# Softmax on negated scores in a windowed-attention encoder kernel on one Trainium2 core

## The chip, the cores and the metric

The kernel runs on one core of one Trainium2 chip. A core has five engines, each with an instruction queue that is worked off in order: TensorE (PE in the profile; its weight loads are shown apart as PEld) multiplies matrices into PSUM, VectorE (DVE) and ScalarE (ACT) do elementwise work and can read PSUM, GpSimd (POOL) does elementwise work on SBUF, and SyncE (SP) issues the transfers. Engines wait for one another through semaphores. The metric is the device time of one execution in microseconds; lower is better.

## The reference

One layer of a hybrid encoder is applied to two batches with the same weights: a prompt of 512 tokens and a sample of 1024 tokens, 1024 channels, float32. After an RMSNorm, one projection gives queries, keys and values for eight heads of 64 channels (two key/value heads, four query heads each) and the inputs of a convolution module. The two branches are joined, projected and added to the input; then comes a gated feed-forward part with 2816 inner channels and a final RMSNorm.

The change lies in the attention. For each block of 128 queries, the keys are those of the block itself and of its neighbours on both sides (384 keys, 256 at the ends of the sequence). Each head has a learned sink logit, which takes part in the softmax's maximum and sum but has no value row:

```
sc = einsum(q, k) * HEAD_DIM ** -0.5 + bias        # bias: relative position, by head
sc = where(|q - k| <= 128, sc, -1e30)
m = maximum(max(sc), sink)
p = exp(sc - m)
denom = sum(p) + exp(sink - m)
o = (p / denom) @ v
```

## The kernel before

All large products are made in a split form: an operand is stored as a rounded high part and the remainder, and three products are added (`hi*hi`, `hi*lo`, `lo*hi`). Making these pairs is most of the work of ACT (the cast to the high part) and of DVE and POOL (the subtraction): `split`, L140 to L145, does it for weights, L211 and L212 for normalised inputs, L548 and L549 for the attention's probabilities.

The program is written as a sequence of stages, partly as generators that are interleaved:

- The prompt's input projections come first, then the sample's. Beside the sample's projections runs the prompt's attention (`prompt`, from about 119 to 250 us), with the depthwise convolution of 31 taps (`conv_items`, L269 to L304, on DVE at L289 and L293, with some taps on ACT at L282 and L285 and POOL at L286).
- The prompt's feed-forward part follows (`ffn_step`; up-projection through `proj`, L250, L251 and L253; three-tap convolution with L775 and L779; gate at L793 to L798; down-projection L813 to L816). Beside it runs the sample's attention (`sample`, from about 400 to 755 us).
- From about 900 us the sample's feed-forward part follows, as products in seven terms over half-size blocks (`prod`, L1039, and `mm_down`, L1352).

`tick` (L228) sets how many steps of a side generator are taken between groups of matmuls, by the rates `RA` to `RE`. This fixes the order in which instructions are given; up to the last stage, a planner then works out each engine's order from the instructions' dependences, their order of writing and estimated durations. In the last stage (from L1202) the order on PE is the written one, and near its end that of SP too.

Attention goes by units: 12 blocks of 128 queries (4 of the prompt, 8 of the sample) times two key/value heads make 24 units of four heads each. A unit's `scores` (L485) takes, for each of its four heads, two matmuls of the scores into a PSUM bank (L502); then one DVE operation (L505) adds the bias, writes the sum to an SBUF tile and leaves the row maximum in a column of `mx`. In the profile L505 shows as a CUSTOM operation and a short read of the accumulator. Then follow, for the four heads together, the negative of the maximum of `mx` and the sink (L512, `negm`) and the sink's exponent (L513, `es`), both on DVE; the four exponentials with `negm` as a bias column, which also leave the row sums in `den` (L515, ACT); the sink's exponential for the four heads in one operation (L517, ACT); the sum of `den` and `es` (L518) and its reciprocal (L519) on DVE; and the scaling of the four tiles on ACT (L523) or on POOL or DVE (L525). `values` (L534) transposes the probabilities on PE (L546), splits them (L548 on ACT, L549 on DVE), multiplies by the values (L560, L561) and stores the result with L568 to L572.

`sinkb` holds the eight sink logits in every partition, `nsink` their negatives; both are made once at the beginning. The small columns (`mx`, `negm`, `den`, `es`) come from a set of 32 small buffers that are given out in turn.

Of the kernel before, what the change touches and what calls it, by code (L numbers as in the profile page):

```python
# [12 lines left out]
AF = mybir.ActivationFunctionType  # L13
ALU = mybir.AluOpType
# [8 lines left out]
GRP = NH // NKV  # L23
# [73 lines left out]
def tile_hybrid_encoder(ctx: ExitStack, tc: tile.TileContext, xs, rel_bias, norm_attn_g, w_in,  # L97
                        attn_sink, conv_dw_w, conv_dw_b, conv_ln_g, conv_ln_b, w_out, norm_ffn_g,
                        w_up, ffn_dw_w, ffn_dw_b, w_down, norm_final_g, onehot, outs):
    nc = tc.nc  # L100
# [11 lines left out]
    def sm(n):  # L112
        return sb.tile([n])

    def bank(job):
        return banks.tile([NT], among=use[job])
# [289 lines left out]
    sinkb = cst.tile([P, NH], F32, name="sinkb")  # L406
    nsink = cst.tile([P, NH], F32, name="nsink")
# [49 lines left out]
    bias = []  # L457
# [15 lines left out]
    def load_q(u):  # L473
        if u < 2 * NB and u not in qt:
            q = sb.tile([GRP, P], F32R)
            i, kv = divmod(u, 2)
            nt, b = divmod(i, 4)
            nc.sync.dma_start(q[:].bitcast(F32), qsd[nt][b, :, kv * GRP:(kv + 1) * GRP, :])
            qt[u] = q

    def window(i):
        G, b = blocks[i]
        return [k for k in (b - 1, b, b + 1) if 0 <= k < G["nb"]]

    def scores(u):  # L485
        i, kv = divmod(u, 2)
        load_q(u)
        if blocks[min(u + 1, 2 * NB - 1) // 2][0] is blocks[i][0]:
            load_q(u + 1)
        G, b = blocks[i]  # L490
        kts = window(i)
        k0, nk = kts[0] * P, len(kts) * P
        off = (kts[0] - b + 1) * P
        q = qt.pop(u)
        mx, negm, den, es = sm(GRP), sm(GRP), sm(GRP), sm(GRP)
        hs = slice(kv * GRP, (kv + 1) * GRP)
        pr = []
        for j in range(GRP):
            h = kv * GRP + j
            sc = bank("attn")  # L500
            for L in range(2):
                nc.tensor.matmul(sc[:, :nk], q[:, j, :], kt[G["g"], kv][L][:, k0:k0 + nk],  # L502
                                 start=(L == 0), stop=(L == 1))
            p = sb.tile([3 * P])
            nc.vector.tensor_tensor_reduce(  # L505
                out=p[:, :nk], in0=sc[:, :nk], in1=bias[h][:, off:off + nk], scale=1.0,
                scalar=-3.0e38, op0=ALU.add, op1=ALU.max, accum_out=mx[:, j:j + 1])
            pr.append(p)
            del sc
            if j == 1:  # L510
                yield 0.0
        nc.vector.scalar_tensor_tensor(negm[:], mx[:], -1.0, nsink[:, hs], op0=ALU.mult, op1=ALU.min)  # L512
        nc.vector.tensor_tensor(es[:], sinkb[:, hs], negm[:], op=ALU.add)  # L513
        for j in range(GRP):
            nc.scalar.activation(pr[j][:, :nk], pr[j][:, :nk], AF.Exp, bias=negm[:, j:j + 1],  # L515
                                 accum_out=den[:, j:j + 1])
        nc.scalar.activation(es[:], es[:], AF.Exp)  # L517
        nc.vector.tensor_tensor(den[:], den[:], es[:], op=ALU.add)  # L518
        nc.vector.reciprocal(den[:], den[:])  # L519
        for j in range(GRP):  # L520
            eng = (SCB if G["g"] == 0 else SCD)[j]
            if eng == "a":
                nc.scalar.activation(pr[j][:, :nk], pr[j][:, :nk], AF.Identity, scale=den[:, j:j + 1])  # L523
            else:
                (nc.vector if eng == "v" else nc.gpsimd).tensor_scalar_mul(pr[j][:, :nk], pr[j][:, :nk], den[:, j:j + 1])  # L525
        units[u] = pr
        yield 0.0
# [51 lines left out]
    def attention(u0, u1, then={}):  # L579
        yield from scores(u0)  # L580
        for u in range(u0, u1):
            if u + 1 < u1:
                yield from scores(u + 1)
            yield from values(u)
            if u in then:
                yield from then[u]
# [698 lines left out]
    pr, second_half = {}, {}  # L1285
# [284 lines left out]
```

## Time and profile before

| what | value |
|---|---|
| median of 3 runs | 1562.63 us (1561.66 to 1564.55) |
| the profiled execution | 1563.92 us, span 1562.1 us |
| granted TensorE clock | 0.998 |
| PE / DVE / ACT / POOL busy | 97% / 77% / 51% / 47% of the span |
| instructions | 20200 |

The span goes from the first to the last instruction of the profiled execution. In rows of the profile, `L505` is line 505 of the kernel; `h<-a,h` names the tiles written and read with their numbers left out; `x24` counts instructions; after the bar stand busy microseconds, the mean of one in ns, and the idle time of the engine just before them with what ended it. In rows of waits, `PE a L561 <- DVE h L549: 1.7, 3, 1.2` says that L561 on PE waited for L549 on DVE 1.7 us in all, three times, at most 1.2 us. In rows in order of time, the first number is the start and the second the duration. A matmul's shown duration overlaps the next one's.

### The profile page before, as it was taken

To read this page: it belongs to the slowest core of one execution; us is meant where nothing else is said; L and a number is where in the kernel's file an instruction comes from. 1 tells how busy PE (TensorE), PEld (TensorE's weight loads), DVE (VectorE), ACT (ScalarE), POOL (GpSimd) and SP (SyncE) were. 2 spreads that over 40 slices of the span, in tenths; PEclk is the share of its full clock that TensorE was granted. 3 is DMA by queue.
4 is the path that set the end of the run, shared out by engine and by line. 5 is a ranking of instruction groups with operands and counts; after the bars stand their busy time and mean duration, and the time that the engine had idled before them with its cause. 6 is when DMAs were issued, how large, how long until landed. Compare 5 with 4: busy or idle time off the path is not lost. (4 is left out here: it accounts for less than half of the span.)

```text
span 1562.1 us, 20200 instructions
## 1 busy us (share of the span) xinstructions
PE 1519.2 (97%) x6909; PEld 1234.5 (79%) x6909; DVE 1200.5 (77%) x1731; ACT 799.2 (51%) x1426; POOL 729.5 (47%) x559
## 2 busy tenths in 40 slices
PE   8899899999998999999999999999999999999998
PEld 6787788887886778888877887888888878788886
DVE  7999868638989996756675768777777777877795
ACT  4634566335565655656554455444444445544364
POOL 7651344238576676656653324555555554000135
PEclk9999999999999999999999999999999999999999
DMA  7573246446331333333657222333333332694642
GB/s 229 157 201 95 87 118 165 130 133 166 108 117 64 108 108 109 99 97 95 212 164 230 82 68 78 111 102 101 101 102 102 101 102 101 206 354 144 219 142 108
DMA packets 209771, 207.62 MB, mean 133 GB/s; under 512 B 11156, under 2 KB 150748, under 8 KB 209541
## 3 DMA queue, kind: packets, MB, share of 16 engines
q1 hardware_dynamic: 209669, 206.35, 42.0%
q8 instruction: 54, 0.88, 0.2%
q14 instruction: 48, 0.39, 0.1%
HBM read 158.84 MB, written 48.51 MB: 133 GB/s over the span
## 5 line engine op out<-in xcount | busy, mean ns | idle before, releaser
L144 POOL TENSOR_TENSOR q<-q,q 128x1024 fp32r<-128x1024 f32 x72 | 175.0, 2436 | 68.8 <-ACT q L143 33.8
L921 POOL TENSOR_TENSOR q<-q,q 128x512 fp32r<-128x512 f32 x82 | 114.0, 1401 | 155.9 <-ACT q L1031 151.4
L250 PE MATMUL u<-h,q 128*128 128x512 f32 x400 | 158.5, 396 | 3.6 <-DVE h L775 2.8
L251 PE MATMUL u<-h,q 128*128 128x512 f32 x400 | 158.6, 396 | 0.6 <-DVE h L212 0.6
L253 PE MATMUL u<-h,q 128*128 128x512 f32 x384 | 151.9, 396 | 2.2 <-POOL q L144 2.2
L1045 PE MATMUL w<-h,q 128*128 128x512 f32 x372 | 147.4, 396 | 3.1 <-ACT h L1126 1.7
L1047 PE MATMUL w<-h,q 128*128 128x512 f32 x372 | 145.9, 392 | 0.6 <-POOL q L921 0.6
L293 DVE SCALAR_TENSOR_TENSOR c<-c,cvw,c 128x512 f32<-128x512 f32 x184 | 138.1, 750 | 2.4
L1046 PE MATMUL w<-h,q 128*128 128x512 f32 x350 | 137.6, 393 | 0.0
L143 ACT CAST q<-q 128x1024 fp32r<-128x1024 f32 x72 | 75.6, 1050 | 77.5 <-POOL q L144 44.6
L918 POOL TENSOR_TENSOR q<-q,q 128x1024 f32<-128x1024 f32 x8 | 23.8, 2989 | 182.9 <-DVE q L918 171.2
L250 PE MATMUL b<-h,q 128*128 128x512 f32 x256 | 102.1, 399 | 2.9 <-DVE d L323 2.9
L1354 PE MATMUL w<-h,h 128*128 128x512 f32 x264 | 103.8, 393 | 0.0
L1356 PE MATMUL w<-h,h 128*128 128x512 f32 x264 | 103.6, 392 | 0.0
L921 DVE TENSOR_TENSOR h<-h,h 128x512 fp32r<-128x512 f32 (+1 forms) x128 | 92.3, 764 | 11.4 <-ACT h L925 9.2
L251 PE MATMUL b<-h,q 128*128 128x512 f32 x256 | 100.7, 393 | 0.0
L253 PE MATMUL b<-h,q 128*128 128x512 f32 x256 | 100.5, 393 | 0.0
L1355 PE MATMUL w<-h,h 128*128 128x512 f32 x244 | 95.9, 393 | 0.0
L921 POOL TENSOR_TENSOR c<-q,c 128x512 fp32r<-128x512 f32 x46 | 71.0, 1557 | 51.8 <-ACT c L1031 51.8
L250 PEld LDWEIGHTS u<-h,q 128*128 128x128 f32 x400 | 75.6, 189 | 20.4 <-DVE h L775 3.3
L925 ACT CAST h<-h 128x512 fp32r<-128x512 f32 x101 | 58.7, 618 | 59.4 <-DVE h L921 27.0
L251 PEld LDWEIGHTS u<-h,q 128*128 128x128 f32 x400 | 75.5, 189 | 16.4 <-DVE h L212 1.6
(457 smaller groups left out, 4278.8 us busy)
## 6 DMA issues: line engine op xcount, KB each, us to landing
q<-in_w_up SPq DMA_DIRECT2D x88, 512.0 KB
h<-in_w_down SPq DMA_DIRECT2D x90, 256.0 KB
ga<-q SPq DMA_DIRECT2D x64, 256.0 KB
h<-ga SPq DMA_DIRECT2D x57, 256.0 KB
q<-in_w_in SPq DMA_DIRECT2D x28, 512.0 KB
q<-in_x_sample SPq DMA_DIRECT2D x15, 512.0 KB
h<-qsd SPq DMA_DIRECT2D x24, 256.0 KB
q<-ga SPq DMA_DIRECT2D x20, 256.0 KB
```

Source lines behind the costliest of these rows:

```text
L144: (nc.vector if dve else nc.gpsimd).tensor_tensor(lo[:], raw[:], hi[:].bitcast(F32), op=ALU.subtract)
L250: nc.tensor.matmul(out, whi[:, kc, :], hi[:], start=(kc == 0), stop=False)
L251: nc.tensor.matmul(out, whi[:, kc, :], lo[:], start=False, stop=False)
L253: nc.tensor.matmul(out, wlo[:, kc, :], hi[:], start=False, stop=(kc == KC - 1))
L293: nc.vector.scalar_tensor_tensor(acc[:], src(t), w(t), acc[:], op0=ALU.mult, op1=ALU.add)
L921: (eng or nc.vector).tensor_tensor(out, a, b, op=ALU.subtract)
L1045: nc.tensor.matmul(out, whi[:, s], hi[:], start=(start and c == 0), stop=False, **go)
L1046: nc.tensor.matmul(out, whi[:, s], lo[:], start=False, stop=False, **go)
L1047: nc.tensor.matmul(out, wlo[:, s], hi[:], start=False, stop=(stop and c == 3), **go)
L1354: nc.tensor.matmul(out, sh[:, c], th[:], start=(p == 0), stop=False)
L1355: nc.tensor.matmul(out, sh[:, c], tl[:], start=False, stop=False)
L1356: nc.tensor.matmul(out, sl[:, c], th[:], start=False, stop=(p == NPAIR - 1))
```

## The change

The row operation now takes the scores with the sign turned: `out = (scores + bias) * -1`, and instead of a running maximum from a large negative constant it keeps a running minimum that starts from the head's column of `nsink`. What it leaves is therefore already the minimum of the negated scores and the negated sink, the value that `negm` had; it goes into a column of `negm`, and `mx` and L512 are gone. The exponential takes its input with a factor of -1. The sink's exponent is no longer added up on DVE (L513 is gone); instead, ScalarE makes `exp(sink + negm)` with a bias column, once for each head, as four one-column operations in place of one of four columns. The sum, the reciprocal and the scaling stay as they were.

```diff
-        mx, negm, den, es = sm(GRP), sm(GRP), sm(GRP), sm(GRP)
-        hs = slice(kv * GRP, (kv + 1) * GRP)
+        negm, den, es = sm(GRP), sm(GRP), sm(GRP)
...
             nc.vector.tensor_tensor_reduce(
-                out=p[:, :nk], in0=sc[:, :nk], in1=bias[h][:, off:off + nk], scale=1.0,
-                scalar=-3.0e38, op0=ALU.add, op1=ALU.max, accum_out=mx[:, j:j + 1])
+                out=p[:, :nk], in0=sc[:, :nk], in1=bias[h][:, off:off + nk], scale=-1.0,
+                scalar=nsink[:, h:h + 1], op0=ALU.add, op1=ALU.min, accum_out=negm[:, j:j + 1])
...
-        nc.vector.scalar_tensor_tensor(negm[:], mx[:], -1.0, nsink[:, hs], op0=ALU.mult, op1=ALU.min)
-        nc.vector.tensor_tensor(es[:], sinkb[:, hs], negm[:], op=ALU.add)
+
         for j in range(GRP):
-            nc.scalar.activation(pr[j][:, :nk], pr[j][:, :nk], AF.Exp, bias=negm[:, j:j + 1],
+            nc.scalar.activation(pr[j][:, :nk], pr[j][:, :nk], AF.Exp, scale=-1.0, bias=negm[:, j:j + 1],
                                  accum_out=den[:, j:j + 1])
-        nc.scalar.activation(es[:], es[:], AF.Exp)
+        for j in range(GRP):
+            h = kv * GRP + j
+            nc.scalar.activation(es[:, j:j + 1], sinkb[:, h:h + 1], AF.Exp, bias=negm[:, j:j + 1])
         nc.vector.tensor_tensor(den[:], den[:], es[:], op=ALU.add)
```

## The prediction

> **What bounds the kernel now.** I read the page first, then busy time by stage, then what TensorE waited for in those stages, and only then the rows of the changed lines. The page gives the engines' shares:
>
> ```profile
> span 1562.1 us, 20200 instructions
> PE 1519.2 (97%) x6909; PEld 1234.5 (79%) x6909; DVE 1200.5 (77%) x1731; ACT 799.2 (51%) x1426; POOL 729.5 (47%) x559
> ```
>
> TensorE is the bound: only 1562.1 - 1519.2 = 42.9 us of the span are left on it. The softmax runs from 119.5 us to about 754 us, so the view of busy time by stage is cut there: the prompt's attention, the two halves of the sample's attention beside the prompt's feed-forward part, and a later stretch without any attention.
>
> ```profile
> 110.00:240.00 130.00, 123.53 (x599) 101.08 (x598) 103.60 (x216) 69.67 (x160) 46.26 (x34) 1.00 0.39 109
> 400.00:600.00 200.00, 192.35 (x877) 155.87 (x876) 182.61 (x323) 119.48 (x235) 133.22 (x87) 0.99 0.31 95
> 600.00:760.00 160.00, 159.44 (x756) 132.08 (x755) 104.13 (x200) 90.51 (x179) 94.28 (x59) 1.00 0.38 119
> ```
>
> The columns are stretch, length, then busy time of PE, PEld, DVE, ACT and POOL. PE is idle 6.5, 7.7 and 0.6 us: a softmax that cost nothing could not win more than some 15 us plus what each stop costs in refilling. VectorE (DVE) is the second engine: idle 26.4, 17.4 and 55.9 us. It is nearly full only in 400 to 600 us (91%). ScalarE (ACT) has 60 us or more to spare in each. Next, what PE waited for in the same three stretches (columns: total, times, longest):
>
> ```profile
> PE a L560 <- ACT h L548: 1.9, 1, 1.9
> ...
> PE a L561 <- DVE q L549: 1.1, 2, 0.8
> PE a L561 <- DVE d L549: 0.2, 1, 0.2
> PE a L546 <- ACT h L523: 0.2, 1, 0.2
> ...
> PE u L250 <- DVE h L775: 2.8, 1, 2.8
> PE a L561 <- DVE h L549: 1.7, 3, 1.2
> PE a L502 <- DVE h L549: 1.0, 1, 1.0
> PE a L502 <- DVE s L505: 0.9, 1, 0.9
> PE a L502 <- DVE h L570: 0.7, 1, 0.7
> PE b L813 <- DVE q L816: 0.4, 1, 0.4
> ...
> PE a L502 <- DVE h L570: 0.5, 1, 0.5
> ```
>
> The first four rows are of 110 to 240 us, the next six of 400 to 600, the last of 600 to 760. No row names L512, L513, L517, L518 or L519, and the one that names L523 is 0.2 us: TensorE hardly ever waits for the softmax's small steps themselves. It waits for DVE work that stood in DVE's queue, 1.3 + 7.5 + 0.5 = 9.3 us in 12 stops. That queue is what the change can shorten.
>
> **The change part by part.** The sum is made against the profiled execution, 1563.92 us (span 1562.1 and 1.8 around it), which is 1.3 us above the median of the runs, 1562.63.
>
> *Two VectorE steps of each of the 24 units go: L512 and L513.* Their rows over the whole run, then each by the same three stretches, L512 first:
>
> ```profile
> L512 DVE SCALAR_TENSOR_TENSOR s<-s,nsink 128x4 f32<-128x4 f32 x24 | 14.1, 587 | 0.2
> L513 DVE TENSOR_TENSOR s<-sinkb,s 128x4 f32<-128x4 f32 x24 | 13.0, 543 | 0.2
> 110.00:240.00 130.00, 2.86 (x7) 1.00 0.39 109
> 400.00:600.00 200.00, 6.29 (x8) 0.99 0.31 95
> 600.00:760.00 160.00, 4.63 (x7) 1.00 0.38 119
> 110.00:240.00 130.00, 2.17 (x7) 1.00 0.39 109
> 400.00:600.00 200.00, 7.44 (x9) 0.99 0.31 95
> 600.00:760.00 160.00, 3.27 (x7) 1.00 0.38 119
> ```
>
> 14.1 + 13.0 = 27.1 us leave DVE. These are four-column operations, yet they take 0.55 us on average, because some are held until a GpSimd operation ends. One such case in the trace, in order of time:
>
> ```profile
> 427.48 2.32 DVE L513 TENSOR_TENSOR s<-sinkb,s 128x4 f32<-128x4 f32 x1
> 429.72 0.68 DVE L794 SCALAR_TENSOR_TENSOR h<-h,h 128x512 f32<-128x512 f32 x1
> ```
>
> An undisturbed one takes about 0.16 us:
>
> ```profile
> 122.23 0.16 DVE L512 SCALAR_TENSOR_TENSOR s<-s,nsink 128x4 f32<-128x4 f32 x1
> 123.02 0.15 DVE L513 TENSOR_TENSOR s<-sinkb,s 128x4 f32<-128x4 f32 x1
> ```
>
> So of the 27.1 us some 24 x 0.31 = 7.4 us are work and 19.7 us are being held. If the held time moves to the next operation, only 7.4 us leave; I take 27.1, since operations that read PSUM, as the two in the next rows, keep means that fit their shapes (683 and 744 ns for 512 columns), and most of what stands next in the queue is of that kind.
>
> *The 96 reductions (L505) take their start value from a per-partition column instead of a constant.* Nearest pair of rows, both reading PSUM and SBUF at 512 columns, the first with such a column, the second with a constant:
>
> ```profile
> L212 DVE SCALAR_TENSOR_TENSOR h<-a,vecs,h 128x512 fp32r<-128x512 f32 x20 | 14.4, 744 | 5.4 <-ACT h L211 5.4
> L328 DVE SCALAR_TENSOR_TENSOR q<-b,q 128x512 fp32r<-128x512 f32 x6 | 4.1, 683 | 4.7 <-ACT q L327 4.6
> ```
>
> 744 - 683 = 61 ns each, 96 x 0.061 = 5.9 us on DVE; the bounds are 0 and twice that. Minimum for maximum and a factor of -1 for 1 change no size and no count: nothing, and the same holds for the -1 in the exponentials. Net, DVE loses 27.1 - 5.9 = 21.2 us: 5.0 - 28 x 0.061 = 3.3 in the first stretch, 13.7 - 36 x 0.061 = 11.5 in the second, 7.9 - 1.7 = 6.2 in the third.
>
> *What that is worth on TensorE.* DVE is in order, and an operation waits the longer in its queue the less idle time DVE has. I let the waits shrink with idle time before over idle time after: 26.4/29.7, 17.4/28.9 and 55.9/62.1, so they fall by 11%, 40% and 10%. Each stop costs PE more than its named idle time, as the restart shows:
>
> ```profile
> 543.46 0.40 PE L815 MATMUL b<-h,d 128*128 128x512 f32 x1
> 543.69 0.39 PE L560 MATMUL a<-h,h 128*128 128x512 f32 x1
> 544.28 0.50 PE L561 MATMUL a<-h,h 128*128 128x512 f32 x1 [0.20 <-DVE h L549]
> ```
>
> The usual step from start to start is 0.23 us, here it is 0.59: a stop named 0.20 costs 0.36, so 0.16 more. With that the stops of the three stretches are worth 1.3 + 3 x 0.16 = 1.8 us, 7.5 + 8 x 0.16 = 8.8 us and 0.7 us, and 0.11 x 1.8 + 0.40 x 8.8 + 0.10 x 0.7 = 0.2 + 3.5 + 0.1 = 3.8 us are gained. Bounds: 0, if these stops have other reasons than a full DVE, and 11.3 us, if all go.
>
> *ScalarE does four one-column exponentials in place of one of four columns.* The rows of the step that goes (with what follows it in the queue) and of the exponentials that have a bias column:
>
> ```profile
> 614.09 0.19 ACT L517 ACTIVATE s<-s 128x4 f32<-128x4 f32 x1
> 614.19 0.60 ACT L797 CAST h<-h 128x512 fp32r<-128x512 f32 x1
> L515 ACT ACTIVATE h<-h,s 128x384 f32<-128x384 f32 x64 | 38.6, 606 | 25.7 <-DVE s L512 25.5
> L515 ACT ACTIVATE h<-h,s 128x256 f32<-128x256 f32 x28 | 13.9, 498 | 9.2 <-DVE s L512 9.2
> ```
>
> Between 256 and 384 columns the exponential grows by 108 ns, 0.84 ns a column, so one column would take about 498 - 215 = 283 ns. The queue moves on 0.09 us before an operation's recorded end (614.19 against 614.28), so each holds the queue 0.19 us: 4 x 0.19 - 0.10 = 0.66 us more a unit, 15.8 us in all; bounds 4 x 0.10 - 0.10 = 0.3 and 4 x 0.283 - 0.10 = 1.03 us a unit (7 to 25 us). ACT's idle time covers it: in the first stretch 60.3 us, of which 7 x 0.66 = 4.6 are taken, which raises PE's two stops behind ACT (2.1 + 2 x 0.16 = 2.4 us) by 8%, 0.2 us. Queued behind the new exponentials are the casts of L548, which PE waits for at L560; that is the place where it would hurt.
>
> [...]
>
> *The order of the chain.* The exponentials no longer wait for L512 (0.59 us on average), and the sum of den and es comes 0.66 us later behind them: the reciprocal keeps its place within 0.1 us, no gain and no loss. Each exponential now needs only its own head's minimum, so ACT's waits for L512 (34.7 us, the two L515 rows above) become shorter waits for L505; PE never waited for them. One small buffer less a unit (mx) frees nothing that anyone waits for.
>
> Sum: -3.8 + 0.2 = -3.6 us: 1560.3 for the profiled execution, **1559.0 us** for the median, 0.2% faster. Differences under 0.2% (3.1 us) I count as none, about what a measurement of this kernel can tell.
>
> **The rivals.** *Nothing changes.* If DVE's held time moves on to other operations, DVE gains 7.4 - 5.9 = 1.5 us in place of 21.2, and TensorE about 0.3 us: 1562.4. For it: L513 was held directly ahead of L794, which has two SBUF inputs as well. Against: the rows of PSUM readers. Also for it: PE is at 97%, and none of its named waits is on the removed steps. [...]
>
> *Slower: the order of the work changes.* The instructions' order on each engine up to about 900 us is not the program's but the planner's; L293, a convolution step, stands between the reductions and L512. Without two DVE steps and with 72 more ACT steps a unit's pieces fall elsewhere. The place is 110 to 760 us; the mechanism is a DVE step that TensorE needs (L775 on the up-projection's bank, L549 or L570 on attention's) planned behind one more long step. One such wait today is 2.8 us (L250 on L775). Three new ones, 8.4 us, turn the gain into +4.8: 1567.4. It decides from the third on. For it: TensorE has few such stops now, so there is more room to get worse than better. Against: DVE has more idle time for each of them.
>
> *Slower: ACT's longer turns.* If in every second unit a cast of L548 that TensorE awaits stands behind the four exponentials, 12 x 0.66 = 7.9 - 3.8 = +4.1 us: 1566.7. It decides from the sixth unit. Against it: one such stop in 24 units now.
>
> **How the numbers follow.** The forecast has 0.40 (1551 to 1559.5, between all stops gone and the 0.2% line). A larger gain by a luckier order has 0.05. No change has 0.22. The changed order has 0.25 and ACT's turns 0.08. Faster is 0.45, same 0.22, slower 0.33. The likeliest case has 1551 to 1560 for its own; the range that holds 8 in 10 reaches down to 1549 (all 11.3 us of stops gone and 2 more) and up to 1572 (nearly five new waits of 2.8 us, 13.4 - 3.6 = 9.8 above the median).
>
> **What the changed profile would show.** DVE busy about 21 us less, 1179, with L512 and L513 gone and L505 at some 610 ns for 384 columns; if it is 551 still, the column is free. ACT busy 24 x (4 x 0.283 - 0.19) = 22.6 us more by recorded durations, 96 exponentials of about 283 ns. PE's named waits for DVE in 400 to 600 us near 4.5 us instead of 7.5. The forecast is wrong if those waits stay although DVE has more idle time, or if new ones of 2 to 3 us stand in the list, above all behind L775, L549 or L548; if stalls only moved, L518, L794 and L795 get longer.

## The result and the profile after

| kernel | median (lowest to highest) | ratio to before, 95% interval |
|---|---|---|
| before, same chip | 1563.59 us (1561.66 to 1565.34) | |
| after | 1575.01 us (1574.59 to 1575.53) | 1.0073 [1.0056, 1.0091] |

The changed kernel is 0.7% slower, 11.4 us, and lies above the predicted range. All times and ratios of this document set a kernel against runs of the kernel before on the same chip. In after the lines move: the scores' matmul is L501 (was L502), the row operation L504 (was L505), the exponentials L513 (was L515), the sink's L517; from L518 on the numbers are the old ones.

The page of after, span and busy times:

```profile
span 1573.7 us, 20193 instructions
PE 1528.0 (97%) x6909; PEld 1243.5 (79%) x6909; DVE 1189.5 (76%) x1683; ACT 816.1 (52%) x1498; POOL 727.5 (46%) x559
```

The span grew by 11.6 us. TensorE is busy 1528.0 instead of 1519.2 us with the same 6909 matmuls: 8.8 us are slower matmuls, and only 2.8 us are more idle time (45.7 against 42.9). DVE lost 11.0 us, not 21.2.

Busy time of after by stage, in the columns of the prediction; the first row is a stage that the prediction did not show (before had 157.53 us of PE there and a clock of 1.00):

```profile
240.00:400.00 160.00, 151.60 (x675) 121.24 (x674) 106.91 (x158) 71.89 (x128) 65.86 (x52) 0.97 0.49 140
400.00:600.00 200.00, 192.04 (x875) 157.40 (x873) 175.59 (x310) 123.41 (x253) 131.23 (x86) 0.98 0.32 101
```

In 400 to 600 us DVE has 24.4 us idle where it had 17.4, as the forecast wanted, and PE gained nothing from it (8.0 us idle, was 7.7). In 240 to 400 us PE lost 5.9 us. What PE waited for in after, from 110 to 900 us, the first rows:

```profile
PE u L250 <- DVE h L775: 6.3, 4, 3.9
PE u L501 <- DMA h<-qsd: 2.8, 2, 1.9
PE a L605 <- DMA q<-cvd: 2.7, 1, 2.7
PE a L605 <- DMA h<-cvd: 2.4, 2, 1.9
PE a L560 <- ACT h L548: 1.8, 3, 0.9
PE a L560 <- ACT q L548: 1.7, 1, 1.7
```

The short stops behind L549, L505 and L570 have gone from the head of the list. In their place stand fewer and longer ones: L775 has four stops instead of one, and the convolution's load (`cvd`) one of 2.7 us. Two places show how they come about. First the longest: one row of GpSimd and DVE's queue in order of time, then TensorE's:

```profile
514.67 2.37 POOL L144 TENSOR_TENSOR q<-q,q 128x1024 fp32r<-128x1024 f32 x1
515.17 0.74 DVE L775 SCALAR_TENSOR_TENSOR h<-u,fw,h 128x511 f32<-128x511 f32 x1
515.83 1.76 DVE L794 SCALAR_TENSOR_TENSOR h<-h,h 128x512 f32<-128x512 f32 x1
517.51 0.74 DVE L293 SCALAR_TENSOR_TENSOR c<-c,cvw,c 128x512 f32<-128x512 f32 x1
518.16 0.61 DVE L504 CUSTOM_DVE_ANT_0 h<-a,h,nsink 128x384 f32<-128x384 f32 x1
518.70 0.08 DVE L504 DVE_READ_ACCUMULATOR2_ANT s<- 128x1 f32 x1
518.70 0.74 DVE L775 SCALAR_TENSOR_TENSOR h<-u,fw,h 128x511 f32<-128x511 f32 x1
```

```profile
515.14 0.52 PE L501 MATMUL a<-q,h 128*128 128x384 f32 x2
519.59 0.77 PE L250 MATMUL u<-h,q 128*128 128x512 f32 x1 [3.93 <-DVE h L775]
520.15 0.63 PE L251 MATMUL u<-h,q 128*128 128x512 f32 x1
520.58 0.63 PE L253 MATMUL u<-h,q 128*128 128x512 f32 x1
...
525.57 0.40 PE L253 MATMUL u<-h,q 128*128 128x512 f32 x1
525.81 0.40 PE L250 MATMUL u<-h,q 128*128 128x512 f32 x1
```

The L775 that frees the up-projection's bank stands in DVE's queue behind L794, L293 and L504, and L794 takes 1.76 us, beside an L144 on GpSimd that ends at 517.04 us; the L794 that the prediction shows took 0.68 us. DVE has no idle time in its six rows, although it has more of it in the stage as a whole. TensorE stops for 3.93 us, and then goes on at half rate: its matmuls start 0.43 us apart (520.15, 520.58) up to 525.3 us, and 0.23 us apart only after that.

The second place is in a stage in which before had no stop over 0.6 us:

```profile
248.52 0.50 PE L560 MATMUL a<-q,h 128*128 128x512 f32 x1 [1.67 <-ACT q L548]
249.76 0.80 PE L561 MATMUL a<-q,h 128*128 128x512 f32 x1 [0.74 <-DVE q L549]
254.13 1.11 PE L605 MATMUL a<-ident,q 128*128 128x128 f32 x4 [2.71 <-DMA q<-cvd]
```

The probabilities of the last prompt unit come late (1.67 and 0.74 us); they lie in a `q` buffer, which the `cvd` load needs next, so the load goes out late (at 251.05 us, in before at 246.16) and PE waits for it too (2.71 us). In before that L560 ran at 245.28 us without a stop. The granted clock (the third column from the end) in these two places, in rows of 10 us:

```profile
240.00:250.00 10.00, 7.55 (x37) 5.65 (x36) 9.40 (x18) 5.15 (x17) 1.44 (x2) 0.95 0.24 79
250.00:260.00 10.00, 7.29 (x22) 5.53 (x23) 6.82 (x14) 5.46 (x11) 2.96 (x4) 0.54 0.68 183
510.00:520.00 10.00, 6.07 (x30) 4.96 (x29) 9.83 (x17) 7.34 (x15) 5.33 (x4) 0.93 0.32 96
520.00:530.00 10.00, 10.00 (x36) 7.98 (x36) 9.78 (x15) 3.67 (x9) 3.63 (x3) 0.73 0.22 74
```

The lowered clock is 0.50 (over the whole of 249 to 259 us and of 518.7 to 525.3 us), so the time at half rate is twice what is missing: 2 x (0.05 + 0.46) x 10 = 10.2 us in the first place and 2 x (0.07 + 0.27) x 10 = 6.8 us in the second. Up to half of that is lost, 5.1 and 3.4 us, on top of the stops themselves (less where PE stands still anyway). Shorter pieces of some 3.4 us each, at 0.50 too, begin near 17, 54, 177 and 798 us; ahead of the last 20 us of the span before has a single one, near 470 us. At up to 1.7 us for each 3.4 us these pieces are enough for the 8.8 us of slower matmuls. Over the whole run the granted clock was 0.989 to 0.991 in after's runs; in the runs of before it lay mostly near 0.995, and the 0.998 of its profile is the top of them.

The rows of the changed operations in after (the row operation, the sink's exponentials, and the sum that follows them):

```profile
L504 DVE CUSTOM_DVE_ANT_0 h<-a,h,nsink 128x384 f32<-128x384 f32 x57 | 34.4, 612 | 16.7 <-PE a L501 7.3 <-PE a L561 4.2 <-DMA catd<-h 3.7
L518 DVE TENSOR_TENSOR s<-s,s 128x4 f32<-128x4 f32 x24 | 12.1, 503 | 1.5 <-ACT s L517 1.3
L517 ACT ACTIVATE s<-sinkb,s 128x1 f32<-128x1 f32 x96 | 27.2, 283 | 0.0
```

The durations are those that were predicted: 612 ns (610), 283 ns (283). So the operations cost what they should, and the loss must come from elsewhere.

### The profile page after: what moved, and what is told of

Same layout as the page of the kernel before. It is cut to its first block, busy times and chain, and to the rows that moved or that the text cites. A ratio compares the mean times of both kernels' runs of the same rounds, so it can differ in the third digit from the quotient of the medians.

```text
span 1573.7 us, 20193 instructions
## 1 busy us (share of the span) xinstructions
PE 1528.0 (97%) x6909; PEld 1243.5 (79%) x6909; DVE 1189.5 (76%) x1683; ACT 816.1 (52%) x1498; POOL 727.5 (46%) x559
## 5 line engine op out<-in xcount | busy, mean ns | idle before, releaser
L144 POOL TENSOR_TENSOR q<-q,q 128x1024 fp32r<-128x1024 f32 x72 | 174.7, 2432 | 89.2 <-ACT q L143 44.5
L250 PE MATMUL u<-h,q 128*128 128x512 f32 x400 | 160.2, 401 | 7.9 <-DVE h L775 6.3
L293 DVE SCALAR_TENSOR_TENSOR c<-c,cvw,c 128x512 f32<-128x512 f32 x184 | 138.0, 750 | 2.7
L250 PE MATMUL b<-h,q 128*128 128x512 f32 x256 | 103.3, 404 | 2.6 <-DVE d L323 2.6
L253 PE MATMUL b<-h,q 128*128 128x512 f32 x256 | 102.7, 402 | 0.0
L251 PE MATMUL b<-h,q 128*128 128x512 f32 x256 | 102.4, 400 | 0.0
L250 PEld LDWEIGHTS u<-h,q 128*128 128x128 f32 x400 | 76.4, 191 | 25.3 <-issue 5.1
```

What stands on the lines that cost most here:

```text
L144: (nc.vector if dve else nc.gpsimd).tensor_tensor(lo[:], raw[:], hi[:].bitcast(F32), op=ALU.subtract)
L250: nc.tensor.matmul(out, whi[:, kc, :], hi[:], start=(kc == 0), stop=False)
L251: nc.tensor.matmul(out, whi[:, kc, :], lo[:], start=False, stop=False)
L253: nc.tensor.matmul(out, wlo[:, kc, :], hi[:], start=False, stop=(kc == KC - 1))
L293: nc.vector.scalar_tensor_tensor(acc[:], src(t), w(t), acc[:], op0=ALU.mult, op1=ALU.add)
```

## The experiments

Theory A: the operations gain a little, as forecast, but the planner lays the whole work out anew, and the new order costs more than they gain. Its rivals put the loss to the operations themselves: to the row operation, which takes 61 ns longer while TensorE waits for its bank, or to ScalarE's four exponentials and the sum that waits for them. In the expectations the rivals carry letters of their own.

### One part of the change at a time

**e1_form**: only the form of the row operation. L512 stays (with a factor of 1 instead of -1), L513 and the single exponential stay.

```diff
-                out=p[:, :nk], in0=sc[:, :nk], in1=bias[h][:, off:off + nk], scale=1.0,
-                scalar=-3.0e38, op0=ALU.add, op1=ALU.max, accum_out=mx[:, j:j + 1])
+                out=p[:, :nk], in0=sc[:, :nk], in1=bias[h][:, off:off + nk], scale=-1.0,
+                scalar=nsink[:, h:h + 1], op0=ALU.add, op1=ALU.min, accum_out=mx[:, j:j + 1])
...
-        nc.vector.scalar_tensor_tensor(negm[:], mx[:], -1.0, nsink[:, hs], op0=ALU.mult, op1=ALU.min)
+        nc.vector.scalar_tensor_tensor(negm[:], mx[:], 1.0, nsink[:, hs], op0=ALU.mult, op1=ALU.min)
```

> The negated form alone: minimum with the sink column as start, scale -1, but L512 (now times +1) and L513 and the one four-column exponential stay. Nothing is left out of the computation. Theory A (the new order of the work, with stops of TensorE that make its granted clock fall, costs the time): the order on TensorE differs from before in a part of its rows, so the time may move either way by up to some 5 us, and what it moves by shows as stops and as granted clock under 0.998. Theory B (the four one-column exponentials on ScalarE cost it): same as before, 1563 +- 3 us. Theory C (the start column makes each L505 longer by 61 ns, and VectorE's 5.9 us come through): 1565 to 1569 us with the clock of before.

**e2_min**: the row operation leaves `negm` itself and L512 is gone; L513 and the single exponential stay.

```diff
-        mx, negm, den, es = sm(GRP), sm(GRP), sm(GRP), sm(GRP)
+        negm, den, es = sm(GRP), sm(GRP), sm(GRP)
...
+                scalar=nsink[:, h:h + 1], op0=ALU.add, op1=ALU.min, accum_out=negm[:, j:j + 1])
...
-        nc.vector.scalar_tensor_tensor(negm[:], mx[:], -1.0, nsink[:, hs], op0=ALU.mult, op1=ALU.min)
```

> The changed row operation alone: L512 and mx are gone, L513 and the one four-column exponential stay. Theory A: its order is new on every engine; the time is 1563 plus what new stops and a lower clock cost, of either sign, and the granted clock tells which: at 0.998 it is 1558 to 1563, at 0.99 it is 1570 to 1576. Theory B: no slower than before, 1559 to 1563. Theory C: 1565 or more at the clock of before.

**e3_es**: only the sink's part. The maximum and L512 stay; L513 is gone, four one-column exponentials take the place of one.

```diff
-        nc.vector.tensor_tensor(es[:], sinkb[:, hs], negm[:], op=ALU.add)
...
-        nc.scalar.activation(es[:], es[:], AF.Exp)
+        for j in range(GRP):
+            h = kv * GRP + j
+            nc.scalar.activation(es[:, j:j + 1], sinkb[:, h:h + 1], AF.Exp, bias=negm[:, j:j + 1])
```

> The sink's term alone: the maximum, mx and L512 stay, L513 goes and four one-column exponentials stand in place of one. Theory B: this part carries the loss, 1572 to 1576 us. Theory A: as for any new order, 1558 to 1576, and the time over 1563 goes with the clock lost: about 1.6 us for each 0.001 under 0.998. Theory C: 1559 to 1563, since L505 keeps its constant.

**e4_order**: the kernel before, with L513 written behind the four exponentials instead of ahead of them. No operation changes.

```diff
-        nc.vector.tensor_tensor(es[:], sinkb[:, hs], negm[:], op=ALU.add)
         for j in range(GRP):
             nc.scalar.activation(pr[j][:, :nk], pr[j][:, :nk], AF.Exp, bias=negm[:, j:j + 1],
                                  accum_out=den[:, j:j + 1])
+        nc.vector.tensor_tensor(es[:], sinkb[:, hs], negm[:], op=ALU.add)
```

> The kernel before with one line moved: L513 is written behind the four exponentials instead of ahead of them. Nothing else changes, and the order on TensorE, GpSimd and SyncE is that of before, row by row. Theory A: 1562 to 1565 us, clock 0.996 to 0.999, the same as before, since TensorE's order and so its stops are the same. Theories B and C: the same as before too. If it is slower by over 0.3%, theory A's tie between the order on TensorE and the time is wrong.

| kernel | median | ratio to before (1563.92 us), 95% interval | places in PE's order that hold another matmul (by line, tile or shape) |
|---|---|---|---|
| e1_form | 1575.64 us | 1.0075 [1.0057, 1.0093] | 1967 of 6909 |
| e2_min | 1567.28 us | 1.0024 [1.0014, 1.0035] | 1974 |
| e3_es | 1582.49 us | 1.0116 [1.0091, 1.0141] | 1953 |
| e4_order | 1562.08 us | 0.9996 [0.9983, 1.0010] | 0 |

Each part alone is slower, and the two parts do not add up to the whole: 11.7 us for the form, 18.6 us for the sink's part, 11.4 us for both together with L512 gone. e3_es takes work away from DVE and loses the most. What the three slow ones share is that more than a quarter of the places in PE's order hold another matmul, in e1_form from the 546th on; e4_order, whose PE, POOL and SP queues are the old ones, is as fast as before. This speaks for the order, but each kernel still changes operations and order at once, and the expectations were not all met: e1_form lost more than any theory had for it (1569 us at most), e3_es lies above every range (1576 at most), and e2_min, with a clock near 0.995 as in before, fits the rival of the longer row operation as well.

### The operations without the new order, and the order without the operations

In the next kernels the order on an engine is written out: between each instruction and the next of the list stands an ordering edge of a kind that makes no wait, so the planner has nothing left to choose there.

```diff
+def keep_order(nc, tc):
+    after = mybir.DependencyInfo(mybir.DependencyClass.NoSync, mybir.DependencyReason.DATA)
...
+        for a, b in zip(order, order[1:]):
+            tc.add_manual_dep(b, a.name, after, reason="kept order")
```

**e5_after_kept**: the changed kernel with the order of the kernel before on all five engines; L512 and L513 drop out of DVE's list, and the four exponentials stand where the one stood. **e6_form_kept** does the same for e1_form, **e7_es_kept** for e3_es.

```diff
 # list for each engine: the order of the kernel before
+        keep_order(nc, tc)   # PE, DVE, ACT, POOL, SP
```

> The changed kernel, every instruction of it, held by ordering edges to the order that the kernel before has on all five engines: L512 and L513 simply missing on VectorE, four one-column exponentials standing where the one stood on ScalarE. The edges add no waits between engines. Theory A (the planner's new order costs the time, the operations do not): the loss goes, 1557 to 1565 us, clock 0.995 or more. Theory B (the operations themselves, ScalarE's longer turns or the longer L505): 1572 to 1578 us, as the changed kernel.

> The negated form with L512, L513 and the one exponential (first experiment), held to the order of before on all engines: each L505 is 61 ns longer and nothing else differs from before. Theory A: 1562 to 1567 us, at most VectorE's 5.9 us above before. Theory C (the longer L505 costs the 12 us of the first experiment): 1573 to 1578 us.

> The sink's term from four one-column exponentials (third experiment), L512 kept, held to the order of before. Theory A: 1559 to 1566 us. Theory B (ScalarE's longer turns cost its 18 us): 1575 to 1585 us.

**e8_before_in_after** turns it round: the operations of the kernel before, with after's order on PE, POOL and SP (DVE and ACT, whose instructions differ, are left to the planner).

```diff
 # kernel before; lists: the order of the changed kernel
+        keep_order(nc, tc)   # PE, POOL, SP
```

> The reverse: the kernel before, every operation of it, held on TensorE, GpSimd and SyncE to the order that the changed kernel has; VectorE and ScalarE are left to the planner. Theory A: slow, 1570 to 1585 us, clock 0.988 to 0.993. Theory B: 1561 to 1565 us, since its operations are those of before.

| kernel | operations | order | median | ratio to before (1563.41 us), 95% interval |
|---|---|---|---|---|
| e6_form_kept | longer row operation | before | 1564.30 us | 1.0002 [0.9992, 1.0011] |
| e7_es_kept | sink's part | before | 1559.72 us | 0.9973 [0.9960, 0.9986] |
| e5_after_kept | the whole change | before | 1551.50 us | 0.9920 [0.9904, 0.9937] |
| e8_before_in_after | before | after | 1588.74 us | 1.0160 [1.0140, 1.0179] |

This settles it for Theory A, though two of its sizes were missed: e5_after_kept is faster than expected (1557 us at least), e8_before_in_after slower (1585 at most). The change itself gains 11.9 us, and e5_after_kept is faster than both kernels; the order that came with it costs 23.5 us (1575.01 - 1551.50), and put upon the operations of before, 25.3 us. The longer row operation costs nothing that can be measured, and four exponentials in place of one sum and one exponential gain 3.7 us. The rest, some 9 us (11.9 - 3.7 with e6's 0.9 counted back), falls to L512's going, by difference and not by a run of its own; the parts need not add up, as a place below shows.

The page of e5_after_kept:

```profile
span 1549.3 us, 20230 instructions
PE 1516.6 (98%) x6909; PEld 1235.9 (80%) x6909; DVE 1181.4 (76%) x1683; ACT 814.0 (53%) x1498; POOL 729.3 (47%) x559
```

Its busy time in 400 to 600 us and in the 10 us around the stop that is looked at below:

```profile
400.00:600.00 200.00, 197.69 (x915) 162.12 (x915) 178.70 (x318) 128.40 (x262) 140.29 (x91) 1.00 0.33 104
470.00:480.00 10.00, 10.00 (x45) 8.22 (x44) 9.90 (x16) 4.83 (x8) 4.05 (x4) 1.00 0.08 28
```

What PE waited for in 400 to 600 us (behind DVE), and the row of the sum:

```profile
PE a L501 <- DVE s L504: 1.2, 1, 1.2
PE a L501 <- DVE h L570: 0.6, 1, 0.6
PE u L250 <- DVE h L775: 0.4, 1, 0.4
```

```profile
L518 DVE TENSOR_TENSOR s<-s,s 128x4 f32<-128x4 f32 x24 | 8.8, 365 | 10.6 <-ACT s L517 10.6
```

DVE has 19.1 us less than before, close to the 21.2 foreseen. PE's idle time is 32.7 us (before 42.9, after 45.7), and its waits for DVE in 400 to 600 us are 2.2 us instead of 7.5. Between after and e5_after_kept lie 24.4 us of span: 13.0 of idle time and 11.4 of matmul time.

Since PE's order is the same in before and in e5_after_kept, each matmul can be set against itself. The lead of e5_after_kept, by the start in before:

```
start in before, us   455.95  488.54  534.05  594.53  775.69  791.15  836.41  987.95
lead, us                0.46    5.68    7.53    9.88    9.80   11.56   12.06   11.92
```

Not all of this lead is the change's. 1.7 us of it arise at one matmul that waits for the `cvd` load (L605, at 785.01 us in before, after a stop of 1.57 us), and there the traces of e4_order, e6_form_kept and e7_es_kept are 1.1 to 1.7 us ahead of before's too; e4_order has every operation of before.

Nearly half of the gain, 5.2 us, comes from one place, the stop of 2.75 us that the prediction quoted as the largest wait for L775. In the kernel before it looked like this, GpSimd, DVE and PE each in order of time, and the row of busy time:

```profile
470.22 2.35 POOL L144 TENSOR_TENSOR q<-q,q 128x1024 fp32r<-128x1024 f32 x1
470.64 2.15 DVE L525 TENSOR_SCALAR h<-h,s 128x384 f32<-128x384 f32 x1
472.71 0.74 DVE L775 SCALAR_TENSOR_TENSOR h<-u,fw,h 128x511 f32<-128x511 f32 x1
470.13 0.62 PE L502 MATMUL a<-q,h 128*128 128x384 f32 x2 [0.95 <-DVE h L549]
473.50 0.61 PE L250 MATMUL u<-h,q 128*128 128x512 f32 x1 [2.75 <-DVE h L775]
473.91 0.63 PE L251 MATMUL u<-h,q 128*128 128x512 f32 x1
```

```profile
470.00:480.00 10.00, 7.12 (x24) 5.48 (x25) 10.00 (x15) 3.02 (x5) 2.57 (x2) 0.83 0.00 0
```

L525 on DVE is held until L144 on GpSimd ends (472.57; L525 ends at 472.79), L775 stands behind it, PE stops, and then its matmuls start 0.43 us apart from 473.50 to 476.90. The clock of 0.83 says the same: 2 x 0.17 x 10 = 3.4 us at half rate, 1.7 us lost. The same L525 in e5_after_kept:

```profile
468.29 0.41 DVE L525 TENSOR_SCALAR h<-h,s 128x384 f32<-128x384 f32 x1
```

With the two operations gone DVE comes to it earlier, it isn't held, and the stretch has neither the stop nor the lower clock. Three kernels with the same order on PE bear this out. Where both operations are still there, in e4_order and e6_form_kept, the stop stands as it was (2.76 us in both, clock 0.83 in 470 to 480 us); in e7_es_kept, where the sink's part alone is changed and L513 alone is gone, it is 0.74 us and the clock 1.00. So the sink's part by itself wins most of this place, and the 9 us put down to L512 by difference are not what L512 would be worth by itself.

The page of e8_before_in_after and its longest waits, in the second fence, show the other side, the new order without the new operations:

```profile
PE 1532.8 (96%) x6909; PEld 1245.5 (78%) x6909; DVE 1187.2 (75%) x1731; ACT 799.4 (50%) x1426; POOL 729.5 (46%) x559
```

```profile
PE a L546 <- ACT h L523: 9.2, 3, 6.0
PE b L813 <- DVE q L816: 5.4, 4, 3.6
PE u L250 <- DVE h L775: 4.6, 2, 4.3
```

PE is idle 58.1 us (1590.9 - 1532.8). The matmuls of L546, L813 and L250 stand too early in PE's queue for what ACT and DVE deliver. This run has DVE and ACT in orders of their own, so it shows that the order by itself is dear, not what it costs to the microsecond.

### Which part of the order, and whether the edges do anything

**e9_first_kept** holds the changed kernel to before's order only for what is written ahead of the prompt's feed-forward part; **e10_second_kept** only from there on; **e11_pe_kept** holds PE's queue alone, over the whole run.

```diff
 # changed kernel; lists: the order of the kernel before
+        keep_order(nc, tc)   # e9: first part; e10: second part; e11: PE alone
```

> The changed kernel with the order of before kept only for what is written ahead of the prompt's feed-forward part (projections, the prompt's attention), on all engines; behind it the planner is free. By the traces the changed kernel lies 11.4 us behind the one with the whole order kept when the last projection matmul starts (360.8 against 349.4 us) and another 11.3 us at the last up-projection matmul (793.2 against 770.5). If both halves of the order cost by themselves: 1575 - 11 = 1564 us, 1560 to 1568. If only the first half's order matters: 1552 to 1556. If only the second's: 1572 to 1576.

> The reverse: the order of before kept only for what is written from the prompt's feed-forward part on, all engines; the planner is free ahead of it. If both halves cost by themselves: 1551.5 + 11.4 = 1563 us, 1560 to 1567, with the stop at the first convolution norm and the low clock near 250 us as in the changed kernel. If only the first half's order matters: 1572 to 1576. If only the second's: 1552 to 1556.

> The changed kernel with the order of before kept on TensorE alone; VectorE, ScalarE, GpSimd and SyncE are left to the planner, which plans them around it. If TensorE's order is what costs: 1550 to 1557 us. If the other queues' order costs (which cast or subtraction stands behind which): 1560 us or more, up to 1590 as in the reverse experiment, where the queues of TensorE, GpSimd and SyncE were given and VectorE and ScalarE were not.

| kernel | median | ratio to before (1563.13 us), 95% interval | regained of the 23.5 us |
|---|---|---|---|
| e9_first_kept | 1564.45 us | 1.0011 [1.0001, 1.0021] | 10.6 |
| e10_second_kept | 1561.34 us | 0.9989 [0.9977, 1.0000] | 13.7 |
| e11_pe_kept | 1557.86 us | 0.9974 [0.9964, 0.9983] | 17.2 |

Both halves of the order cost, about the same, and they add up (10.6 + 13.7 = 24.3). So it isn't one bad place. PE's order alone brings back three quarters of it; the rest lies in the orders of the other queues, so e11_pe_kept falls between its two expectations (up to 1557 us, and from 1560). In e9_first_kept L775's stops, which lie in the second half, are after's own; in e10_second_kept the place of the first half is as in after (PE's waits from 110 to 900 us, first e9_first_kept, then e10_second_kept):

```profile
PE u L250 <- DVE h L775: 6.3, 4, 3.9
```

```profile
PE a L605 <- DMA q<-cvd: 3.0, 1, 3.0
PE a L560 <- ACT q L548: 1.7, 1, 1.7
```

**e12_after_own** is the control: the changed kernel with its own order written out by the same edges on all five engines.

```diff
 # changed kernel; lists: its own order
+        keep_order(nc, tc)   # PE, DVE, ACT, POOL, SP
```

> The changed kernel with its own order on all five engines written out by the same kind of ordering edges that gave 1551.5 us with the order of the kernel before. If the order is what differs (Theory A), the edges by themselves do nothing and this run gives 1575 (1573 to 1577). If the edges themselves make a kernel faster, by removing or moving waits and register steps between the instructions, it comes out near 1563 or below, and the 23.5 us put down to the order shrink by as much.

Measured: 1576.29 us (1572.38 to 1577.21), 1.0077 [1.0060, 1.0094]. The edges by themselves gain nothing, and its longest stop is the same as after's:

```profile
519.33 0.77 PE L250 MATMUL u<-h,q 128*128 128x512 f32 x1 [3.93 <-DVE h L775]
```

How the loss splits into idle time and slower matmuls is not fixed: with the same order on every engine the trace of e12_after_own has six half-rate pieces of 3.4 us where after's has nine, 2.3 us less of matmul time and 4.0 us more of idle time.

What stays open is why the planner arrives at the worse order: whether the two dependences that are gone, the one column more of the row operation, or its estimate for 72 more ScalarE operations tips it. e1_form, with no operation more or less, changes the order as much as e3_es does, so the count is not needed. None of this was tried inside the planner.

## Why the prediction was wrong, point by point

*The step that failed* is the assumption under the forecast that the pieces of a unit keep their places, with the order's change left to a rival at 0.25. The rival had the mechanism right, down to the line: L775, on the up-projection's bank, planned behind one more long step. Its argument against ("DVE has more idle time for each of them") was the error. A stage's idle time says nothing of the queue at one place: DVE was full from 510 to 520 us in after, in a stage where it had 7 us more to spare, and L794, the step ahead of that L775, took 1.76 us beside GpSimd.

*The rival's price* was too low, 8.4 us for three stops of 2.8 against a measured 23.5. It counted stops behind L775 alone. After has L775's four (6.3 us, before 2.8), but also the late load of `cvd` with the L560 and L561 ahead of it (5.1 us, before none at that place), and behind the long ones a half-rate stretch each.

*The worth of DVE's time on TensorE*, 3.8 us, was mis-sized: 11.9 us with the order kept. The place was right (400 to 600 us gives 9.4 of the 12 us of lead), and so was the first link, a shorter DVE queue. Two numbers were off. The restart of a stop was priced at 0.16 us from one stop of 0.20 us; the pair of stops at 470 us, 3.7 us by name, gave back 5.2 us. The half-rate stretch behind such a stop, 1.7 us there, is in no term of the sum, although the row of 400 to 600 us that it quotes shows a clock of 0.99. And the waits do not shrink in proportion to idle time: that one vanished as a whole, because it hung on one meeting with a GpSimd operation, which is luck and not a share of idle time. The upper bound of 11.3 us, "if all go", lies near the measured 11.9 partly by chance, as it counts neither the half-rate stretch nor the stop at `cvd`.

*VectorE, -21.2 us*: near with the order kept (-19.1), half in after (-11.0). The two operations took their 27.1 us along; the 61 ns are 61 at 384 columns (551 to 612) and 59 at 256. But the held time came back in part at other small operations: L518 is 365 ns in e5_after_kept and 503 in after, before 279. That is the "held time moves on" of the first rival; its outcome, no change, did not come.

*ScalarE*: right. 96 exponentials of 283 ns make 27.2 us, 22.6 more than the one L517; as they overlap, ACT's busy time grew by 16.9. The price on TensorE (0.2 us) cannot be told apart within e7_es_kept, where the whole of the sink's part gains 3.7 us; the rival of ACT's longer turns is refuted by it for the order of before. With the order kept the small exponentials lay beside the path: e7_es_kept, which has all 96 of them, is faster than before (1559.72 against 1563.41 us).

*TensorE at 97%*, with none of its named waits on the removed steps, was an argument for no change. It doesn't hold: with the order kept the whole change was worth 11.9 us, since PE's stops hang on DVE's queue (its waits for DVE in 400 to 600 us fell from 7.5 to 2.2 us).

*The signs that were named* held in part. New stops "of 2 to 3 us" were to be looked for "above all behind L775, L549 or L548": after has one of 3.9 us behind L775, one of 1.7 behind L548, and one of 2.7 behind `cvd`, which wasn't named. The other sign would have misled: PE's waits for DVE in 400 to 600 us fell to 5.1 us, near the forecast 4.5, while PE's idle time there stayed as it was, because 2.3 us of waits for ACT came in (before 0.2).

## What to carry to other kernels

Where a planner lays out the instructions, an edit of a few small operations is two changes, the operations and a new order of everything; hold the order fixed and measure them apart before judging the edit, since here they were worth -11.9 and +23.5 us. Price a stop of TensorE at its idle time and a refill (0.16 us at a stop of 0.20 us here), and count on up to 1.7 us or a multiple more for a half-rate stretch behind a long one: in the traces of before and after it came with four of the five stops of over 2.5 us (3.93, 2.75, 2.71 and 2.63 us, but not 2.92), and with some shorter ones (0.87 us at 17 us in after). And in a nearly full queue look for the single step that a long neighbour delays, not at the stage's average.

## What was not expected of the hardware

Ahead of the last 20 us of the span, the lowered clock of before and after (0.50 each time) came in whole pieces. After stops of 0.95 and 2.75 us (before, 470 us) it lasted 3.4 us, after one of 3.93 us 6.8 us, after 1.67, 0.74 and 2.71 us close together 10.2 us: one, two and three times 3.4 us, always with steps of 0.43 instead of 0.23 us between matmuls of 512 columns. After a single stop of 1.24 us (before, 518 us) there was none, and none either after one of 2.92 us (before, 52 us, clock 1.00 from 50 to 60 us):

```profile
52.15 0.50 PE L250 MATMUL b<-h,q 128*128 128x512 f32 x1 [2.92 <-DVE d L323]
```

Whether a stop sets it off is not a matter of its length alone. At the beginning, where both kernels have the same instructions and the same stops, one goes on at half rate and the other doesn't (after, then before):

```profile
17.39 0.80 PE L250 MATMUL u<-h,q 128*128 128x512 f32 x1 [0.87 <-DVE h L212]
```

```profile
17.27 0.50 PE L250 MATMUL u<-h,q 128*128 128x512 f32 x1 [0.86 <-DVE h L212]
```

The same shows with the same operations in the same order on every engine: a stop of 1.95 us at `cvd` in after (797 us) is followed by a half-rate piece (clock 0.92 and 0.91 in 790 to 810 us), one of 2.51 us at the same matmul in e12_after_own (799 us) by none (1.00). So two runs of the same order can differ by whole pieces, at up to 1.7 us each: nine in after's trace, six in that of e12_after_own. And behind a stop of 1.88 us at 163 us there is one in e4_order (clock 0.83), where the same stop in before has none (1.00 from 160 to 170 us).

The other surprise is how far a held operation reaches: a scaling of 384 columns that took 2.15 us at the side of a GpSimd operation of 2.35 us cost TensorE some 4.1 us, more than its own length: 2.4 us of standing still and 1.7 us of the half-rate stretch (the other 1.1 us of the 5.2 belong to the stop just ahead of it, at L502).
